# Seven half-token products for eight in the last gate and the output projection, with weights summed by accumulating DMAs

## The chip, the cores and the metric

The kernel runs on one core of a Trainium2 chip. The metric is device time in microseconds (us) of one execution, the median of several. TensorE (PE in the profile, its weight loads PEld), VectorE (DVE), ScalarE (ACT), GpSimd (POOL) and the DMA queues (issued by SP or by POOL) run side by side; each works through its own instructions in order.

## The reference

Two layers, 512 tokens, model width 1024. The part that the change touches is the gates, the merge and the output projection of each layer:

```python
h = _rmsnorm(x, g_mix[l])
proj = h @ w_in[l]                 # 4096 gate columns, then the inputs of the four branches
...                                # y_a conv module, y_b, y_c, y_d three attentions
ys = jnp.stack([y_a, y_b, y_c, y_d], axis=2)
branch = jnp.einsum('bsnc,ncd->bsnd', ys, w_branch[l])
gates = jax.nn.sigmoid(gate_pre.reshape(bsz, seq, N_BRANCH, D_MODEL) + gate_b[l])
mixed = jnp.sum(gates * branch, axis=2)
x = x + mixed @ w_out[l]
x = x + _conv_ffn(_rmsnorm(x, g_ffn[l]), w_up[l], ffn_conv_w[l], ffn_conv_b[l], w_down[l])
```

All of it is float32. The result has the shape of x.

## The kernel before

**Precision.** A float32 product is made of three: each operand is split into an upper part (hi, a rounded copy made by ScalarE) and a lower part (lo, the difference, made by VectorE), and TensorE adds hi x hi, hi x lo and lo x hi in PSUM (`prod`, L243 to L245). So every weight costs one ScalarE copy (L222) and one VectorE subtraction (L224), besides its DMA (L218).

**Weights.** They are packed on the host in units of 128 x 1024 floats (512 KB) in the order of use. `weights` (L197) loads a unit into one of two raw buffers, splits it into one of three hi and three lo buffers, and `unit` (L228) hands it out; the next unit is traced one ahead (`LOOK`), with a priority that lets it go before other work. A raw buffer is free again when the lower part has been made, a hi or lo buffer when TensorE has used it.

**Layout.** Activations lie transposed: channels on the partitions, the 512 tokens along the row. A block (`block`, L256) is one unit: 8 tiles of 128 input channels, three matmuls of 128 x 128 by 512 tokens each, 24 in all.

**The order in a layer.** Projections for the three attentions and the conv module come first, then four gates in the order 1, 2, 3, 0 (`ORDER`), then the output projection, the FFN's up-projection and its down-projection. Attention and the conv module run as generators in a side queue; `tick` (L844) takes one step of each of them, between blocks, so that their small matmuls stand among the large ones. In the third gate the queue still holds the end of attention and of the conv module; it is emptied after that gate.

**A gate** (`gates`, L797). For each of eight 128-channel tiles: a block, a multiplication by RB (the reciprocal norm of each token, L806), a tanh on ScalarE (L808). Two tiles later the branch product of 6 matmuls (`branch`, L818) and, on VectorE, (tanh + 1) times it (L835), which is added to the tile `mixed[d]` (L836), on POOL except for the last two tiles of the last gate. In the last gate `mixed[d]` is split at once into mh and ml (L840, L841), which are the moving operands of the output projection.

**The output projection** (`layer`, L1210). Eight blocks; the first two stop after six of eight input tiles and take the last two later, so that the last gate's tail is covered. Each result is added to the residual loaded from memory (`update`, L877: L882), stored as the new residual (L883), and turned into the FFN's input (`norm_tile`, L289: xh L300, xl L301, squares L309, their sum L310).

The down-projection already uses seven products for eight, with sums of weights that VectorE makes during the FFN and that go through memory (`weight_sums`, L973; L978 to L984). The gate and the output projection do not.

## Time and profile before

| | |
|---|---|
| median of 3 runs | 1558.79 us (1558.77 to 1559.04) |
| span of the profiled execution, first to last instruction | 1556.7 us |
| TensorE busy | 1550.7 us |
| weight loads busy | 1287.2 us |
| VectorE busy | 1235.9 us |
| ScalarE busy | 834.7 us |
| POOL busy | 174.8 us |
| DMA | 244.86 MB, 157 GB/s |

The page gives the span of the profiled execution and not its time outside the span; the median of the runs is 2.1 us above it. A matmul's duration in the profile includes its way through the array, and matmuls overlap, so a busy TensorE is not yet one at its peak: the distance from one start to the next is what counts. Weight loads run beside the matmuls. In a row on a group stand the line, engine, operation, what is written and read, shapes, count, then busy us and mean ns of one, then the idle time of that engine just ahead and what ended it. A row of the timeline begins with its start and its length in us.

### The profile page before, as it was taken

To read this page: it belongs to the slowest core of one execution; us is meant where nothing else is said; L and a number is where in the kernel's file an instruction comes from. 1 tells how busy PE (TensorE), PEld (TensorE's weight loads), DVE (VectorE), ACT (ScalarE), POOL (GpSimd) and SP (SyncE) were. 2 spreads that over 40 slices of the span, in tenths; PEclk is the share of its full clock that TensorE was granted. 3 is DMA by queue.
4 is the path that set the end of the run, shared out by engine and by line. 5 is a ranking of instruction groups with operands and counts; after the bars stand their busy time and mean duration, and the time that the engine had idled before them with its cause. 6 is when DMAs were issued, how large, how long until landed. Compare 5 with 4: busy or idle time off the path is not lost.

```text
span 1556.7 us, 20353 instructions
## 1 busy us (share of the span) xinstructions
PE 1550.7 (100%) x7122; PEld 1287.2 (83%) x7122; DVE 1235.9 (79%) x2102; ACT 834.7 (54%) x1420; POOL 174.8 (11%) x304
## 2 busy tenths in 40 slices
PE   9999999999999999999999999999999999999999
PEld 8888888888888888888888888888888888888887
DVE  6689988765689997796676899887656899977964
ACT  6778767333445443364457787672434444443643
POOL 0102002122001111100001020022120111111000
PEclk9999999999999999999999999999999999999999
DMA  7632222222645555576555422223226667655674
GB/s 236 192 93 87 83 81 82 95 98 93 215 162 203 192 187 187 202 238 211 188 181 184 117 72 87 74 76 108 95 95 211 194 221 238 202 203 191 219 231 165
DMA packets 103382, 244.86 MB, mean 157 GB/s; under 512 B 27504, under 2 KB 29424, under 8 KB 103280
## 3 DMA queue, kind: packets, MB, share of 16 engines
q1 hardware_dynamic: 89392, 196.37, 39.6%
q0 software_dynamic: 13600, 46.67, 8.5%
q8 instruction: 56, 0.92, 0.2%
q10 hardware_dynamic: 288, 0.52, 0.1%
q14 instruction: 46, 0.38, 0.1%
HBM read 202.63 MB, written 35.66 MB: 153 GB/s over the span
## 4 chain that ended last, share of the span: by engine, by line
PE 94%; DVE 3%; ACT 3%; issue 0%; ACTq 0%; DVEq 0%
PE mm L243 22%; PE mm L244 22%; PE mm L245 22%; PE aux L1048 3%; PE aux L1047 3%; PE aux L1046 3%; PE mm L467 2%; PE mm L469 2%; PE mm L468 2%; PE mm L1047 2%; PE mm L1048 2%; PE mm L1046 2%; PE aux L760 2%; PE aux L737 2%; PE aux L467 1%; PE aux L469 1%
## 5 line engine op out<-in xcount | busy, mean ns | idle before, releaser
L222 ACT ACTIVATE w_hi<-w_raw 128x1024 fp32r<-128x1024 f32 (+1 forms) x305 | 318.6, 1045 | 382.6 <-PE mm L244 218.9
L243 PE MATMUL mm<-xh,w_hi 128*128 128x512 f32 x1280 | 499.5, 390 | 0.0
L244 PE MATMUL mm<-xl,w_hi 128*128 128x512 f32 x1280 | 498.6, 390 | 0.0
L245 PE MATMUL mm<-xh,w_lo 128*128 128x512 f32 x1280 | 498.6, 390 | 0.0
L224 DVE TENSOR_TENSOR w_lo<-w_raw,w_hi 128x1024 fp32r<-128x1024 f32 (+1 forms) x305 | 368.7, 1210 | 83.4 <-ACT w_hi L222 81.3
L245 PEld LDWEIGHTS mm<-xh,w_lo 128*128 128x128 f32 x1280 | 240.3, 188 | 50.7
L243 PEld LDWEIGHTS mm<-xh,w_hi 128*128 128x128 f32 x1280 | 240.3, 188 | 49.1
L244 PEld LDWEIGHTS mm<-xl,w_hi 128*128 128x128 f32 x1280 | 240.3, 188 | 48.7
L836 POOL TENSOR_TENSOR mx<-mx,t 128x512 f32<-128x512 f32 x44 | 66.9, 1530 | 428.0 <-DVE t L835 327.1
L405 DVE SCALAR_TENSOR_TENSOR cv<-cv,prm 128x512 f32<-128x512 f32 x120 | 93.8, 781 | 0.7
L915 DVE TENSOR_TENSOR U<-mm,RB 128x512 f32<-128x512 f32 x88 | 60.0, 686 | 34.9 <-PE mm L245 34.8
L918 ACT ACTIVATE cy<-U,prm 128x512 f32<-128x512 f32 x88 | 70.7, 807 | 30.1 <-DVE U L915 29.9
L806 DVE TENSOR_TENSOR t<-mm,RB 128x512 f32<-128x512 f32 x64 | 43.9, 686 | 47.0 <-PE mm L245 46.8
L467 PE MATMUL mm<-w_hi,xh 128*128 128x512 f32 x192 | 76.4, 398 | 0.4 <-DVE V L595 0.4
L468 PE MATMUL mm<-w_lo,xh 128*128 128x512 f32 x192 | 75.0, 390 | 0.0
L469 PE MATMUL mm<-w_hi,xl 128*128 128x512 f32 x192 | 74.8, 390 | 0.0
L724 ACT ACTIVATE e<-e,rl 128x256 f32<-128x256 f32 (+2 forms) x96 | 57.3, 597 | 21.8 <-DVE rl L723 21.5
L920 DVE SCALAR_TENSOR_TENSOR cy<-U,prm,cy 128x512 f32<-128x512 f32 x88 | 65.5, 746 | 1.3
L919 DVE SCALAR_TENSOR_TENSOR cy<-U,prm,cy 128x512 f32<-128x512 f32 x88 | 65.3, 744 | 0.6 <-ACT cy L918 0.6
L924 ACT ACTIVATE fth<-cy 128x512 f32<-128x512 f32 x44 | 27.8, 632 | 64.1 <-DVE cy L920 64.0
L984 POOL DMA_DIRECT2D sums<-t x44 | 23.9, 544 | 339.4 <-DVE t L978 311.3
L717 ACT ACTIVATE e<-e,nm 128x256 f32<-128x256 f32 (+2 forms) x96 | 57.6, 600 | 2.7
(300 smaller groups left out, 2605.2 us busy)
## 6 DMA issues: line engine op xcount, KB each, us to landing
w_raw<-W SPq DMA_DIRECT2D x223, 512.0 KB, 3.5
quad<-W POOLq DMA_DIRECT2D x44, 512.0 KB, 5.3
w_raw<-W SPq DMA_DIRECT2D x66, 256.0 KB, 3.6
sums<-t POOLq DMA_DIRECT2D x44, 256.0 KB, 3.2
sums<-quad POOLq DMA_DIRECT2D x44, 256.0 KB, 3.8
w_raw<-sums SPq DMA_DIRECT2D x44, 256.0 KB, 3.8
w_raw<-sums SPq DMA_DIRECT2D x22, 512.0 KB, 4.4
res<-xn SPq DMA_DIRECT2D x24, 256.0 KB, 2.0
```

Of the source, the lines that this page charges most:

```text
L222: w = nc.scalar.activation(hi[:, s], raw[:, s], AF.Copy)
L224: nc.vector.tensor_tensor(lo[:, s], raw[:, s], hi[:, s].bitcast(F32), ALU.subtract)
L243: mm(ps, lhsT=wh, rhs=xh, start=start, stop=False)
L244: mm(ps, lhsT=wh, rhs=xl, start=False, stop=False)
L245: self.last_mm = mm(ps, lhsT=wl, rhs=xh, start=False, stop=stop)
L405: self.after_mm(v.scalar_tensor_tensor(acc, u[:, t:t + S], w(t), acc, ALU.mult, ALU.add))
L467: mm(pss[b], lhsT=self.Xh[k][:, t], rhs=hi[:, s], start=k == 0, stop=False)
L468: mm(pss[b], lhsT=self.Xh[k][:, t], rhs=lo[:, s], start=False, stop=False)
L469: self.last_mm = mm(pss[b], lhsT=self.Xl[k][:, t], rhs=hi[:, s], start=False, stop=k == KT - 1)
L1046: mm(ps, lhsT=x[0], rhs=w[0][:, cols], start=start, stop=False, skip_group_check=again)
L1047: mm(ps, lhsT=x[0], rhs=w[1][:, cols], start=False, stop=False, skip_group_check=again)
L1048: self.last_mm = mm(ps, lhsT=x[1], rhs=w[0][:, cols], start=False, stop=stop, skip_group_check=again)
```

## The change

The matrix product of the last gate (weights of gate 0, named `0`) and that of the output projection (`o`) are each cut in two halves of output channels, `a` and `b`, which gives four groups: `0a`, `0b`, `oa`, `ob`. In a group the weights are a 2 x 2 block matrix (output half by input parity) and the input is one too (input parity by token half). Seven products of sums of such blocks (S1 to S4, A11, A12, A22) replace the eight plain block products. Each product is one 512 KB unit of weights and 24 matmuls over 256 tokens.

- The sums of weights are made by DMA: a chain tile is loaded with one block and three others are added to it one after the other by accumulating DMAs from POOL (`grow`), and the splits for S3, S2 and S4 are taken between; A22's raw tile grows into that for S1. The two chain tiles (a, b) belong to the new pool `outp`.
- The sums of inputs are made by VectorE: `input_forms` reads the residual again, applies the gain and makes four forms from each of four pairs of tiles, beside the third gate; `mixed_forms` does it for each pair of tiles of `mixed`.
- The results are recombined by ScalarE copies and VectorE adds (`seven_copy`, `seven_sum`), then `last_gate` applies RB and tanh, `last_out` adds the residual and goes on to `norm_tile`.
- `LAST` is the order of all products and the two branch units. The first three of the output projection do half of their input tiles, then the other half.
- The pool of attention closes after the third tile of the third gate instead of after that gate, and `outp` opens there. `th` has four buffers instead of three. The adds of `mixed` in the last gate go to VectorE from tile 4 on.
- The whole residual (two tiles to a buffer, shared with the sums) is loaded after the last branch products.

```diff
+LAST = [('0a', n) for n in ('S3', 'A11', 'A22', 'S2', 'A12', 'S1')] + [
+    ('0b', 'S3'), ('0a', 'S4'), ('0b', 'A11'), ('branch', 0), ('0b', 'A22'), ('0b', 'S2'), ('0b', 'A12'), ('0b', 'S1'),
+    ('branch', 1), ('0b', 'S4'),
+    ('oa', 'S3'), ('oa', 'A11'), ('oa', 'A12'), ('oa', 'A22'), ('oa', 'S2'), ('ob', 'S3'), ('oa', 'S1'), ('ob', 'A11'),
+    ('oa', 'S4'), ('ob', 'A22'), ('ob', 'S2'), ('ob', 'A12'), ('ob', 'S1'), ('ob', 'S4')]
+CHAINS = {'0a': ('0b', 'S3', 'A22'), '0b': ('oa', 'A11', 'S2'), 'oa': ('ob', 'S3', 'A12'), 'ob': (None, '', '')}
...
+    def grow(self, raw, src):
+        self.nc.gpsimd.dma_start(raw, src, accum_op=ALU.add)
+    def chain_start(self, l, key):
+        raw = self.op.tile([P, 1024], F32, name="chain", tag=f"chain{key[1]}", bufs=1)
+        self.nc.sync.dma_start(raw, self.quarters[l][key, 1, 0])
+        self.chains[key] = raw
+    def seven_unit(self, l, key, n):
...
+        if n[0] == 'S':
+            raw = self.chains[key] if n != 'S1' else self.others[key]
+        else:
+            raw = self.wpool.tile([P, 1024], F32, name="w_raw", tag="w_raw", bufs=2)
+            nc.sync.dma_start(raw, q[key, int(n[1]) - 1, int(n[2]) - 1])
...
+        nc.scalar.activation(hi, raw, AF.Copy)
+        nc.vector.tensor_tensor(lo, raw, hi.bitcast(F32), ALU.subtract)
+        add = {'S3': (1, 1), 'A22': (1, 0), 'S2': (0, 1)}.get(n)
+        if add:
+            self.after.append(lambda: self.grow(raw, q[(key,) + add]))
+        if n == 'A22':
+            self.others[key] = raw
+        key2, at, then = CHAINS[key]
+        if n == at:
+            self.chain_start(l, key2)
+        if n == then:
+            self.after.append(lambda: self.grow(self.chains[key2], q[key2, 0, 0]))
+        return hi, lo
...
-        (v if n == ORDER[3] and d >= 6 else nc.gpsimd).tensor_tensor(m, m, t, ALU.add)
-        if n == ORDER[3]:
-            mh = self.op.tile([P, S], F32R, name=f"mh{d}", tag=f"mh{d}", bufs=1)
-            ml = self.op.tile([P, S], F32R, name=f"ml{d}", tag=f"ml{d}", bufs=1)
-            nc.scalar.activation(mh, m, AF.Copy, scale=0.5)
-            v.scalar_tensor_tensor(ml, m, 0.5, mh.bitcast(F32), ALU.mult, ALU.subtract)
-            self.MH.append((mh, ml))
+        (v if n == ORDER[3] and d >= 4 else nc.gpsimd).tensor_tensor(m, m, t, ALU.add)
+        if n == ORDER[3] and d % 2 == 1:
+            self.mixed_forms(d // 2)
...
+    def form_sums(self, t, b11, b12, b21, b22):
+        t1, t2, t3, t4 = (t[:, n * 256:(n + 1) * 256] for n in range(4))
+        p = self.nc.vector.tensor_tensor
+        p(t3, b12, b22, ALU.subtract)
+        p(t1, b11, b12, ALU.subtract)
+        p(t2, t3, b11, ALU.subtract)
+        p(t4, b21, t2, ALU.add)
...
+    def mixed_forms(self, j):
...
+        for h, l, s in ((th, tl, t), (bh[:, :256], bl[:, :256], x[:, :256]), (bh[:, 256:], bl[:, 256:], y)):
+            nc.scalar.activation(h, s, AF.Copy, scale=0.5)
+            v.scalar_tensor_tensor(l, s, 0.5, h.bitcast(F32), ALU.mult, ALU.subtract)
...
+    def seven_part(self, key, n, w, js, e):
+        ps = self.seven_bank(key, n)
+        o = ps[:, e * 256:(e + 1) * 256]
+        for j in js:
+            s = slice((2 * j + e) * P, (2 * j + e + 1) * P)
+            xh, xl = self.seven_x(key, n, j)
+            for i, (a, x) in enumerate(((w[0], xh), (w[0], xl), (w[1], xh))):
...
+                self.last_mm = self.nc.tensor.matmul(o, lhsT=a[:, s], rhs=x, start=start, stop=j == 3 and i == 2,
+                                                     skip_group_check=True)
...
+    def seven(self, key, n, done):
+        w = self.unit()
+        for e in range(2):
+            self.seven_part(key, n, w, range(4), e)
...
+        if n in ('S3', 'A11'):
+            self.seven_copy(key, n)
+            return
+        if not (key == 'ob' and n == 'S1'):
+            self.seven_sum(key, n)
+        done(key, n)
...
+    def last_gate_and_out(self):
...
+        for key, n in steps[:at]:
+            if key == 'branch':
+                bu = self.unit()
+                for d in range(4 * n, 4 * n + (4, 2)[n]):
+                    self.branch(ORDER[3], d, bu, self.ths[d])
+                    self.tick()
+                continue
+            self.seven(key, n, self.last_gate)
+        for d in (6, 7):
+            self.branch(ORDER[3], d, bu, self.ths[d])
+        for q in range(4):
+            self.load_residual(q)
...
+        for key, n in steps[at:at + 3]:
+            ws.append(self.unit())
+            for e in range(2):
+                self.seven_part(key, n, ws[-1], (0, 1), e)
+        for (key, n), w in zip(steps[at:at + 3], ws):
+            for e in range(2):
+                self.seven_part(key, n, w, (2, 3), e)
...
+        for key, n in steps[at + 3:]:
+            self.seven(key, n, self.last_out)
...
-                for n in ORDER[:3]:
-                    self.gates(n)
+                for n in ORDER[:2]:
+                    for _ in self.gates(n):
+                        pass
+                third = self.gates(ORDER[2])
+                next(third)
+                while any(g is not conv for g in self.side):
+                    self.tick()
+            with tc.tile_pool(name="outp", bufs=1, reuse_waits="tile") as self.op:
+                self.chains, self.others = {}, {}
+                self.input_forms()
+                self.chain_start(l, '0a')
+                self.after.append(lambda: self.grow(self.chains['0a'], self.quarters[l]['0a', 0, 0]))
+                for _ in third:
+                    pass
                 while self.side:
                     self.tick()
-            with tc.tile_pool(name="outp", bufs=1, reuse_waits="tile") as self.op:
-                self.gates(ORDER[3])
...
+                self.last_gate_and_out()
                 self.broadcast_norm()
```

More of the change, by code (lines that the diff above doesn't have):

```diff
@@ L88, in weight_units @@
                 units.append(('branch', (n, d // 4), 1024))
-    for d in range(8):
-        units.append(('out', d, 1024))
+    units.extend(('quarter', (key, r, c), 1024) for key in ('0a', '0b', 'oa', 'ob') for r in range(2) for c in range(2))
+    units.extend(('branch', (ORDER[3], h), 1024) for h in range(2))
     for i in range(NF):
@@ L201, in weights @@
             n, pieces = self.w_list[self.w_emitted]
+            after, self.after = self.after, []
+            with self.tc.high_priority(offset=ahead):
+                for f in after:
+                    f()
+            if n == 'seven':
+                with self.tc.high_priority(offset=ahead):
+                    self.w_ready.append(self.seven_unit(*pieces))
+                self.w_emitted += 1
+                continue
             with self.tc.high_priority(offset=ahead):
@@ new lines, in seven_x @@
+    def seven_x(self, key, n, j):
+        form = {'S1': 0, 'S2': 1, 'S3': 2, 'A22': 3}.get(n)
+        if form is not None:
+            return [t[:, form * 256:(form + 1) * 256] for t in (self.forms[j] if key[0] == '0' else self.mforms[j][0])]
+        if key[0] == 'o':
+            c = ('A11', 'A12', 'S4').index(n)
+            return [t[:, c * 256:(c + 1) * 256] for t in self.mforms[j][1]]
+        k, h = {'A11': (0, 0), 'A12': (1, 0), 'S4': (1, 1)}[n]
+        return [t[2 * j + k][:, h * 256:(h + 1) * 256] for t in (self.Xh, self.Xl)]
@@ L1157, in run @@
                         quads.append(src)
-                    else:
-                        self.w_list.append((n, lambda src=src: [src]))
+                    elif kind == 'quarter':
+                        quarters[a] = src
+                    elif kind == 'branch' and a[0] == ORDER[3]:
+                        branches.append(src)
+                    else:
+                        (held if kind == 'up' else self.w_list).append((n, lambda src=src: [src]))
+                for key, n in LAST:
+                    if key == 'branch':
+                        self.w_list.append((1024, lambda src=branches[n]: [src]))
+                    else:
+                        self.w_list.append(('seven', (l, key, n)))
+                self.w_list.extend(held)
+                self.quarters.append(quarters)
                 self.quads.append(quads)
```

167 lines of the change are left out of this document (141 added, 26 removed).

## The prediction, made before the result was known

> **What bounds the kernel now.** I read the page first (busy time, chain), then busy time by stretch, then matmul starts, then the groups of instructions of the two stretches that the change rewrites, then the DMA.
>
> ```profile
> span 1556.7 us, 20353 instructions
> PE 1550.7 (100%) x7122; PEld 1287.2 (83%) x7122; DVE 1235.9 (79%) x2102; ACT 834.7 (54%) x1420; POOL 174.8 (11%) x304
> PE 94%; DVE 3%; ACT 3%; issue 0%; ACTq 0%; DVEq 0%
> ```
>
> TensorE is never idle and carries 94% of the chain that ended last. Time can go only where TensorE has less to stream, and only as long as no other engine becomes late. The profile's span is 1556.7 us; the median of the runs is 1558.79, so 2.1 us lie around the span. I work out differences and put them on 1558.8.
>
> ```profile
> core 0: us, PE busy (x) PEld busy (x) DVE busy (x) ACT busy (x) POOL busy (x), PEclk, DMA share, GB/s
> 276.00:342.00 66.00, 66.00 (x303) 54.69 (x303) 48.88 (x77) 24.28 (x32) 16.37 (x11) 1.00 0.30 102
> 342.00:390.00 48.00, 48.00 (x214) 39.74 (x213) 23.99 (x29) 16.29 (x21) 8.59 (x6) 1.00 0.30 95
> 390.00:434.00 44.00, 44.00 (x196) 36.44 (x195) 27.03 (x35) 18.95 (x26) 1.47 (x10) 1.00 0.61 202
> 434.00:460.00 26.00, 26.00 (x117) 21.52 (x116) 23.95 (x37) 10.40 (x13) 3.26 (x6) 1.00 0.52 182
> ```
>
> These are, in layer 0, the third gate, the last gate, the output projection and the start of the FFN; layer 1 has the same stages. VectorE (DVE) is half idle in the last gate, 61% busy in the output projection and 92% busy in the FFN, where TensorE still does not wait. The granted clock is 1.00 throughout.
>
> **The products: what TensorE saves.** Before, the last gate and the output projection are 8 blocks each of 24 matmuls over 512 tokens: 384 in a layer. After, four groups of seven products, each 24 matmuls over 256 tokens: 672 in a layer. Half as wide is not half as long by itself, because each matmul brings its own 128x128 weight load. The attention's value products are the nearest case that the trace has: 256 wide, each with its own load, several in a row.
>
> ```profile
> 82.89 0.39 PE L243 MATMUL mm<-xh,w_hi 128*128 128x512 f32 x1
> 83.12 0.39 PE L244 MATMUL mm<-xl,w_hi 128*128 128x512 f32 x1
> 83.35 0.39 PE L245 MATMUL mm<-xh,w_lo 128*128 128x512 f32 x1
> 83.57 0.63 PE L760 MATMUL aux<-pt,V 128*128 128x256 f32 x4
> 84.05 0.27 PE L737 MATMUL aux<-cst,e 128*128 128x128 f32 x1
> ...
> 83.12 0.19 PEld L245 LDWEIGHTS mm<-xh,w_lo 128*128 128x128 f32 x1
> 83.35 0.65 PEld L760 LDWEIGHTS aux<-pt,V 128*128 128x128 f32 x4
> ```
>
> The duration (0.39) is a latency; what counts is the distance of starts. From 82.89 to 83.57 are three 512-wide starts, 0.227 us each. From 83.57 to 84.05 are four 256-wide ones, 0.120 each. So 384 x 0.227 = 87.2 us become 672 x 0.120 = 80.6: 6.6 us less in a layer, 13.2 in both. The ends: at exactly half of 0.227 the products take 76.3 and save 10.9 (21.8 in both). If all went as the widest gap that these rows allow (three distances inside the x4 row take 0.35, so the fourth takes 0.13), they take 87.4 and save nothing. I take 0.120, the mean of a run of four; weight loads start 0.11 to 0.12 apart there, so the load is what paces them.
>
> In a sentence apart: the Trainium skill, TensorE: Matmul & The Clock Gate, Back-to-back issue gap, gives N/2.4 + 2.5 ns at full clock, that is an estimated 216 ns for 512 and 109 ns for 256, and by it the layer would save 82.9 - 73.4 = 9.5 us; the rows above show 227 and 120, 11 ns more at either width, and the measurement decides.
>
> **The VectorE sum.** Durations of its instructions and of the two it exchanges work with:
>
> ```profile
> L224 DVE TENSOR_TENSOR w_lo<-w_raw,w_hi 128x1024 fp32r<-128x1024 f32 x9 | 11.0, 1224 | 1.6 <-ACT w_hi L222 1.5
> L806 DVE TENSOR_TENSOR t<-mm,RB 128x512 f32<-128x512 f32 x7 | 4.8, 692 | 12.1 <-PE mm L245 12.1
> L835 DVE SCALAR_TENSOR_TENSOR t<-th,mm 128x512 f32<-128x512 f32 x7 | 4.8, 682 | 0.0
> L841 DVE SCALAR_TENSOR_TENSOR ml<-mx,mh 128x512 fp32r<-128x512 f32 x5 | 3.5, 693 | 10.4 <-ACT mh L840 10.4
> ...
> L301 DVE SCALAR_TENSOR_TENSOR xl<-xn,prm,xh 128x512 fp32r<-128x512 f32 x7 | 5.2, 747 | 0.8 <-ACT xh L300 0.8
> ...
> L222 ACT ACTIVATE w_hi<-w_raw 128x1024 fp32r<-128x1024 f32 x8 | 8.5, 1060 | 15.6 <-PE mm L244 15.6
> L808 ACT ACTIVATE th<-t,gbh 128x512 f32<-128x512 f32 x8 | 5.7, 712 | 0.0
> ...
> 285.77 0.43 DVE L745 TENSOR_TENSOR pt<-aux,pt 128x256 fp32r<-128x256 f32 x1
> 319.12 2.35 DVE L224 TENSOR_TENSOR w_lo<-w_raw,w_hi 128x1024 fp32r<-128x1024 f32 x2
> 388.68 1.30 POOL L836 TENSOR_TENSOR mx<-mx,t 128x512 f32<-128x512 f32 x1 [5.52 <-DVE t L835]
> 389.31 1.22 DVE L836 TENSOR_TENSOR mx<-mx,t 128x512 f32<-128x512 f32 x1
> 389.67 0.39 PE L243 MATMUL mm<-mh,w_hi 128*128 128x512 f32 x1
> 393.62 0.68 DVE L836 TENSOR_TENSOR mx<-mx,t 128x512 f32<-128x512 f32 x1
> 395.01 0.69 DVE L841 SCALAR_TENSOR_TENSOR ml<-mx,mh 128x512 fp32r<-128x512 f32 x1 [0.70 <-ACT mh L840]
> ```
>
> Two w_lo back to back take 2.35, so instructions follow each other some 0.09 closer than their durations: 1.14 us at 1024 wide, 0.60 at 512, 0.34 at 256. What is added in a layer: 12 more weight splits (28 products and 2 branch units for 18 units), 16 small subtractions for the forms of the gate's input and 16 for those of the mixed sum, the recombination (three 512-wide instructions in each of four groups), four adds that leave POOL; the eight mh/ml splits become wider ones. By the rates above: 13.7 + 10.9 + 4.6 (lower parts of the input forms) + 7.2 + 2.4 + 3.6, some 42 us of VectorE in a layer. Stage by stage:
>
> Input forms (third gate): 4 x (4 x 0.34 + 1.14) = 10.0 us on VectorE, 8 x 0.71 + 4 x 1.06 = 9.9 on ScalarE. The stretch 276 to 342 leaves 17 and 42 us free: nothing on the path; without that cover the 10 us would fall on the next stage. The 2.1 MB that it loads once more meet a DMA share of 0.30.
>
> Attention's pool closing in the third gate:
>
> ```profile
> 293.14 0.69 DVE L780 TENSOR_TENSOR yl<-yf,yh 128x512 fp32r<-128x512 f32 x1
> ...
> 295.48 0.69 DVE L806 TENSOR_TENSOR t<-mm,RB 128x512 f32<-128x512 f32 x1 [0.99 <-PE mm L245]
> ```
>
> The last result of attention stands at 293.8, before the third block of this gate is read at 295.48. That gate's first branch needs it anyway, so emptying the side queue there drains nothing: 0.
>
> The last gate's second half is where the sum does not close. Between the first branch product and the second half of the output's first product (which needs the forms of the last mixed pair), TensorE has seven further branch products (7 x 6 x 0.227 = 9.5), five products of 24 x 0.120 = 2.9 (14.4), the first halves of three (36 x 0.120 = 4.3) and three matmuls (0.4): 28.6 us. In that time VectorE must do eight gate multiplies of L835's kind (8 x 0.60 = 4.8), four adds (2.4), the 16 subtractions (5.4), four 1024-wide lower parts (4.6), three pairs of 256 and 512 wide (2.8), seven weight splits (8.0; the ring of three lets none be made sooner), three recombinations (1.8) and four RB multiplies (2.4): 32.2. So 3.6 us are missing in each layer even if VectorE never idles: 7.2 in both. Before, the same hand-over had room: the last ml ends at 395.7, while 36 matmuls from 389.7 last to 397.9. Ends for this term: 0, if TensorE's own slower pitch absorbs it; 7.7 a layer by rival two.
>
> In the output projection VectorE has, for a group, 7 x 1.14 + 3 x 0.60 + 4 x 0.60 (residual) + 4 x 0.66 (xl) + 4 x 0.60 (sqacc) = 17.2 us in 7 x 2.88 = 20.2: 85%, below the 92% at which the FFN runs without a wait. ScalarE: 7 x 1.06 for splits, three copies and eight xh and sq at 0.71 at most: 15.2. I cost both at 0. Without cover each late split costs at most its 1.14. After the last product two half-width adds replace one add; the FFN's first block reads that tile in its last quarter: 0.
>
> The waits that are added, and the queues: each accumulating DMA waits on POOL for both halves of the split that reads its tile. Behind it on POOL stand the gate's adds for tiles 0 to 3, used two products later, and the next accumulation. On SP, the residual loads into XR2 and XR3 wait until the last forms are read (they share those tiles); a weight load or a store that stands behind them waits too, at most the 3.6 us above again. The buffers of raw weights: of two, one is held from A22 to S1, three products; loads, splits and that hold fill about 28 of 40 buffer-us in a group: 0.
>
> ```profile
> DMA packets 3384, 8.90 MB, mean 202 GB/s; under 512 B 384, under 2 KB 384, under 8 KB 3381
> w_raw<-W SPq DMA_DIRECT2D x8, 512.0 KB, 4.2
> ...
> quad<-W POOLq DMA_DIRECT2D x44, 512.0 KB, 5.3
> ```
>
> The first two rows are of 390 to 434. The trace has no accumulating DMA. Nearest is POOL's plain 512 KB load, 5.3 us to landing. From the split of S3 to that of S2 three products pass, 8.6 us, less 2.3 for the split itself: 6.3, so 5.3 fits; twice that (10.6) fits only with the two products of lead that the ring allows (5.8). Between 0 and 4.3 us each, seen three times in a group; I take 0, the row it is nearest to, and leave the rest to rival three.
>
> Sum: 1558.8 - 13.2 + 7.2 = 1552.8 us.
>
> **Rivals.**
> One, the narrow matmuls go at half of 0.227. Then 21.8 is saved, the stretch above is shorter on TensorE by 159 x 0.0065 = 1.0, so 4.6 a layer comes back: 1558.8 - 21.8 + 9.2 = 1546.2. Against it: the run of four.
>
> Two, no measurable change: VectorE's backlog is larger. The rows at 388.68 and 389.31 show an add, which takes 0.68 at 393.62, take 1.22 on VectorE while POOL runs its own; four such meetings in the stretch are 2.2 us. At its end come two hops over ScalarE (two half-wide tanh, by L808's 0.71 an estimated 0.4 each, then the upper part of the last form, 1.06) with little left for VectorE to do: 1.9. 3.6 + 2.2 + 1.9 = 7.7 a layer: 1558.8 - 13.2 + 15.4 = 1561.0. For it: every term has a row. Against it: the hops can be filled with weight splits.
>
> Three, slower: the DMA becomes the bound of the output projection. In 40.3 us it must move some 15 weight transfers (7.9 MB), residual loads and stores (4.2) and the FFN's first quads (1.0): 13.1 MB, 325 GB/s. The stretch before moved 8.90 MB at a share of 0.61 in 44 us, 331 GB/s if full. If the seven accumulations in it (3.7 MB) cost double because the destination is read as well, 16.8 MB need 50.7 us, 10.4 more a layer: 1552.8 + 20.8 = 1573.6. It decides from about 1.3 times the price of a plain load, where the stage grows by 3 us and the gain is gone. Against it: a part is prefetched in the last gate, where the share was 0.30, and stores can trail into the FFN, so half the price (1563) is as likely as all of it.
> The Trainium skill, Collectives: The Full Stack, The bandwidth ceiling, says that an adding transfer is slow for its two source reads, not for the add, and so runs at about half the rate of a copy; no run here shows it yet, and by that rule this rival's time is the one above.
>
> Four, the change does not do what it says: loads of 0.19 us stay in front of each narrow matmul, 672 x 0.19 = 128 us, 1640. The four starts in 0.48 us speak against it.
>
> **How the numbers follow.** Forecast 0.39, rival one 0.11, two 0.21, three 0.26, four 0.01; 0.02 for anything else. A measurement of this kernel tells 0.2%, 3.1 us, from no change, so faster is below 1555.7 and slower above 1561.9. The forecast and rival one are faster; some of the forecast's spread (a backlog of 5 a layer) lies within: faster 0.46, same 0.21, slower 0.33. The range goes from rival one to rival three, 1546 to 1573; the forecast's own is 1549 to 1557.
>
> **What would show it.** Starts of the 256-wide products 0.120 apart (0.113: rival one). VectorE over 95% busy from the first branch of the last gate on, and TensorE waiting for the forms of the last mixed pair, some 3.6 us. No wait of ScalarE's w_hi for a DMA, accumulations landing within about 6 us; w_hi waiting for the chain tile and DMA slices at 9 in the output projection would be rival three. I am wrong if VectorE's order differs from need so that splits come ahead of forms, or if the accumulation is much dearer than a load.

## The result, and the profile after

The changed kernel takes 1608.61 us (median of 4 runs, 1607.47 to 1609.09) against 1558.91 beside it: ratio 1.0317, 95% interval 1.0303 to 1.0332. The forecast was 1552.8, its range ended at 1573, so it was wrong in sign and by 56 us. First the page after: span, busy times, shares of the chain that ended last.

```profile
span 1607.0 us, 21849 instructions
PE 1564.0 (97%) x7698; PEld 1319.2 (82%) x7698; DVE 1322.6 (82%) x2236; ACT 898.4 (56%) x1516; POOL 199.5 (12%) x332
PE 80%; DVE 11%; ACT 4%; DMA 2%; issue 2%; POOL 0%; SPq 0%; ACTq 0%; DVEq 0%
```

TensorE falls from 94 to 80% of the chain, VectorE rises from 3 to 11 and DMA appears. Busy time by stretch in layer 0 (third gate, last gate, output projection, start of the FFN):

```profile
core 0: us, PE busy (x) PEld busy (x) DVE busy (x) ACT busy (x) POOL busy (x), PEclk, DMA share, GB/s
276.00:342.00 66.00, 62.06 (x283) 51.19 (x282) 56.38 (x95) 31.61 (x42) 17.57 (x13) 0.97 0.55 165
342.00:396.00 54.00, 52.24 (x388) 49.38 (x387) 42.15 (x52) 29.72 (x44) 15.13 (x14) 1.00 0.69 161
396.00:442.00 46.00, 41.09 (x294) 38.89 (x293) 34.88 (x49) 23.74 (x33) 5.65 (x15) 0.89 0.72 184
442.00:484.00 42.00, 33.63 (x156) 27.28 (x156) 32.44 (x49) 16.85 (x21) 3.27 (x6) 0.96 0.56 185
```

TensorE was busy in every microsecond of these stretches before; now 3.9, 1.8, 4.9 and 8.4 us are missing, and the granted clock is below 1.00 in three of them. Two accounts of the 50.3 us between the spans (1607.0 - 1556.7) close, the second to some 2 us:

| place, by the starts of matmuls | before | after | us |
|---|---|---|---|
| start to the first product of the mixed sum, layer 0 | 389.7 | 395.1 | +5.4 |
| from there to the down-projection, layer 0 | 283.3 | 301.9 | +18.6 |
| down-projection of layer 0 to the first product of the mixed sum, layer 1 | 491.7 | 496.7 | +5.0 |
| from there to the down-projection, layer 1 | 283.3 | 304.5 | +21.2 |

By kind, over all pairs of successive matmuls: a distance within 12 ns of the even pitch (0.227 us at 512 wide, 0.120 at 256) counts as work, one within 12 ns of the pitch at half clock (0.427 at 512 wide, as the rows of the last section show it, 0.213 at 256) as halved clock, and what goes beyond the even pitch otherwise as waiting. Waiting grew by some 49 us, halved clock by some 12; less the 13.2 saved that is some 48. A distance can be near 0.427 or 0.213 by chance, so the rule is sure only where the granted clock is below 1.00; that is 0.986 on the mean here and 0.999 before. The waits stand in the third gate (4.1 us at 323.9, 3.7 in layer 1), between 375 and 413 (some 10 in each layer), at 441.8 (5.3; 3.3) and at 475.8 (3.3; 4.2).

**Third gate.** TensorE stood before the convolution's second transposes (instructions of VectorE and TensorE; the two rows above the line of dots are of the kernel before, the rest of the one after):

```profile
313.23 1.27 DVE L425 TENSOR_SCALAR ms<-mv 128x4 f32<-128x4 f32 x1
316.51 0.16 DVE L277 SCALAR_TENSOR_TENSOR rln<-rs_q,rln 128x4 f32<-128x4 f32 x1
...
318.03 1.26 DVE L482 TENSOR_SCALAR ms<-mv 128x4 f32<-128x4 f32 x1
319.20 0.41 DVE L903 TENSOR_TENSOR sums<-xf 128x256 f32<-128x256 f32 x1
325.53 1.21 DVE L929 TENSOR_TENSOR form<-sums,form 128x1024 fp32r<-128x1024 f32 x1
327.44 0.16 DVE L334 SCALAR_TENSOR_TENSOR rln<-rs_q,rln 128x4 f32<-128x4 f32 x1
328.23 0.69 PE L500 MATMUL aux<-cst,cv 128*128 128x128 f32 x2 [3.94 <-DVE cv L491]
```

The serial chain for a reciprocal root on 128x4 elements took 3.4 us before (313.23 to 316.67) and takes 9.6 now (318.03 to 327.60): input sums, lower parts and weight splits stand between its links.

**Mixed hand-over.** Busy time in stretches of the kernel after (columns as above; the first reaches from the end of the first branch product to the first matmul that needs the lower part of the last form), then two instructions of VectorE:

```profile
368.55:410.49 41.94, 36.30 (x227) 32.02 (x225) 38.81 (x57) 21.31 (x31) 8.72 (x8) 0.92 0.58 141
372.20:405.00 32.80, 28.25 (x194) 25.23 (x192) 32.80 (x49) 17.99 (x27) 5.59 (x5) 0.97 0.63 161
400.00:405.00 5.00, 2.48 (x11) 1.76 (x11) 5.00 (x10) 2.28 (x5) 0.00 (x0) 0.79 0.54 193
405.00:410.00 5.00, 4.40 (x18) 3.78 (x17) 3.18 (x5) 2.95 (x3) 0.40 (x1) 0.53 0.00 0
...
408.07 1.23 DVE L272 TENSOR_TENSOR w_lo<-w_raw,w_hi 128x1024 fp32r<-128x1024 f32 x1 [1.82 <-ACT w_hi L271]
409.22 1.22 DVE L949 SCALAR_TENSOR_TENSOR mform<-sums,mform 128x1024 fp32r<-128x1024 f32 x1
```

VectorE has no idle time from 372.2 to 405, while TensorE waits for it (28.25 of 32.80 us busy). At the end the order works against it too: the lower part of the last form (409.22) stands behind a weight split that waits 1.82 us for ScalarE, which waits for a buffer that TensorE holds. From 405 to 410 the clock is 0.53.

**Hand-over to the FFN.** Two waits of 440 to 480 after, the end of the norm's chain before (450.68) and after (476.70), and TensorE's wait for a bank of PSUM:

```profile
PE mm L300 <- ACT w_hi L245: 5.1, 1, 5.1
ACT w_hi L245 <- DMA w_raw<-W: 6.1, 1, 6.1
...
450.68 0.68 DVE L277 SCALAR_TENSOR_TENSOR RB<-rs_q,RB 128x512 f32<-128x512 f32 x1
476.70 0.69 DVE L334 SCALAR_TENSOR_TENSOR RB<-rs_q,RB 128x512 f32<-128x512 f32 x1
479.28 0.47 PE L300 MATMUL mm<-xh,w_hi 128*128 128x512 f32 x1 [3.14 <-DVE U L1181]
```

The FFN's first product stands ahead of the last two output products on TensorE, and its weight is late. It is late because of what is loaded beside it. The stretch from 432 to 444 and the load of this weight, in the kernel after and below the dots in e11, which has no accumulating loads:

```profile
432.00:444.00 12.00, 10.05 (x84) 9.85 (x83) 9.37 (x13) 5.87 (x8) 2.19 (x11) 1.00 0.96 284
w_raw<-W SPq DMA_DIRECT2D x1, 512.0 KB, 11.3
...
432.00:444.00 12.00, 11.44 (x92) 10.91 (x91) 11.46 (x16) 7.00 (x9) 0.00 (x0) 1.00 0.40 133
w_raw<-W SPq DMA_DIRECT2D x1, 512.0 KB, 3.5
```

The weight is issued at 434.6 and lands 11.3 us later; in e11 it is issued at 435.0 and lands in 3.5. In the kernel after, the two loads of the FFN's quads (512 KB each, the weights whose sums the down-projection needs) stand behind the accumulating loads on POOL's queue and start at 433.6 and 434.1, beside the last accumulation and the stores; in e11 they start at 406.3 and 406.9. So the DMA share is 0.96 there, against 0.38 in the same stretch of the kernel before.

The norm's chain ends 22.4 us after the last output product (454.95), before 18.4 (432.97), and the FFN's fifth product waits for it.

### The profile page after: what moved, and what is told of

The parts are those of the page before. It is cut to its first block, busy times and chain, and to the rows that moved or that the text cites. A ratio compares the mean times of both kernels' runs of the same rounds, so it can differ in the third digit from the quotient of the medians.

```text
span 1607.0 us, 21849 instructions
## 1 busy us (share of the span) xinstructions
PE 1564.0 (97%) x7698; PEld 1319.2 (82%) x7698; DVE 1322.6 (82%) x2236; ACT 898.4 (56%) x1516; POOL 199.5 (12%) x332
## 3 DMA queue, kind: packets, MB, share of 16 engines
q1 hardware_dynamic: 91696, 200.57, 39.4%
## 4 chain that ended last, share of the span: by engine, by line
PE 80%; DVE 11%; ACT 4%; DMA 2%; issue 2%; POOL 0%; SPq 0%; ACTq 0%; DVEq 0%
PE mm L302 15%; PE mm L300 15%; PE mm L301 15%; PE aux L972 6%; PE aux L1312 2%; PE aux L1313 2%; PE aux L1314 2%; PE mm L524 2%; PE mm L526 2%; PE mm L525 2%; DVE w_lo L247 2%; PE mm L1313 2%; PE mm L1312 2%; PE mm L1314 2%; PE aux L817 2%
## 5 line engine op out<-in xcount | busy, mean ns | idle before, releaser
L300 PE MATMUL mm<-xh,w_hi 128*128 128x512 f32 x1152 | 451.3, 392 | 15.4 <-ACT w_hi L245 8.2
L302 PE MATMUL mm<-xh,w_lo 128*128 128x512 f32 x1152 | 450.8, 391 | 0.6 <-DVE w_lo L247 0.5
L301 PE MATMUL mm<-xl,w_hi 128*128 128x512 f32 x1152 | 450.5, 391 | 0.0
L245 ACT ACTIVATE w_hi<-w_raw 128x1024 fp32r<-128x1024 f32 (+1 forms) x273 | 284.9, 1044 | 288.5 <-PE mm L301 104.4
L247 DVE TENSOR_TENSOR w_lo<-w_raw,w_hi 128x1024 fp32r<-128x1024 f32 (+1 forms) x273 | 329.7, 1209 | 88.1 <-ACT w_hi L245 84.9
L300 PEld LDWEIGHTS mm<-xh,w_hi 128*128 128x128 f32 x1152 | 217.4, 189 | 61.0 <-ACT w_hi L245 8.6
L302 PEld LDWEIGHTS mm<-xh,w_lo 128*128 128x128 f32 x1152 | 217.2, 189 | 47.3 <-DVE w_lo L247 1.8
L301 PEld LDWEIGHTS mm<-xl,w_hi 128*128 128x128 f32 x1152 | 217.4, 189 | 43.7 <-DVE xl L358 0.2
L272 DVE TENSOR_TENSOR w_lo<-w_raw,w_hi 128x1024 fp32r<-128x1024 f32 x32 | 41.8, 1306 | 23.9 <-ACT w_hi L271 23.7
L972 PE MATMUL aux<-mform,w_hi 128*128 128x256 f32 x256 | 53.9, 309 | 5.8 <-DVE mform L949 2.1
```

The costliest lines, as they stand in the source:

```text
L245: w = nc.scalar.activation(hi[:, s], raw[:, s], AF.Copy)
L247: nc.vector.tensor_tensor(lo[:, s], raw[:, s], hi[:, s].bitcast(F32), ALU.subtract)
L300: mm(ps, lhsT=wh, rhs=xh, start=start, stop=False)
L301: mm(ps, lhsT=wh, rhs=xl, start=False, stop=False)
L302: self.last_mm = mm(ps, lhsT=wl, rhs=xh, start=False, stop=stop)
L972: self.last_mm = self.nc.tensor.matmul(o, lhsT=a[:, s], rhs=x, start=start, stop=j == 3 and i == 2, skip_group_check=True)
```

## Experiments

All are edits of the changed kernel; the ratio is to the kernel before, run beside it. e8, e10, e11 and e17 leave out work that the result needs: they measure what it costs and are no candidates.

| run | edit | us | ratio (95%) |
|---|---|---|---|
| e1_gate7 | the gate alone in seven | 1566.25 | 1.0038 (1.0025 to 1.0051) |
| e2_out7 | the output alone in seven | 1591.86 | 1.0207 (1.0191 to 1.0222) |
| e3_order | FFN behind the last product | 1608.16 | 1.0306 (1.0289 to 1.0323) |
| e4_conv | convolution's chain first | 1609.28 | 1.0320 (1.0305 to 1.0336) |
| e5_own | own tile for A22 | 1609.17 | 1.0324 (1.0309 to 1.0340) |
| e6_own_order | e3 and e5 | 1603.75 | 1.0291 (1.0276 to 1.0306) |
| e7_forms_mid | forms written later | 1606.21 | 1.0302 (1.0284 to 1.0319) |
| e8_nosums | mixed forms without their sums | 1588.04 | 1.0185 (1.0170 to 1.0200) |
| e9_behind | forms behind the convolution | 1623.17 | 1.0411 (1.0395 to 1.0426) |
| e10_plain_load | plain loads, nothing is added | 1602.57 | 1.0278 (1.0262 to 1.0293) |
| e11_no_load | no accumulating loads | 1593.44 | 1.0225 (1.0208 to 1.0242) |
| e12_gate7_behind | e1 and e9 | 1581.42 | 1.0141 (1.0125 to 1.0156) |
| e13_gate7_split | e1, forms split 2 and 2 | 1558.18 | 0.9995 (0.9985 to 1.0004) |
| e14_gate7_split_a11 | e13, A11 first | 1568.23 | 1.0051 (1.0033 to 1.0069) |
| e15_half_norm | e6, norm by half tiles | 1601.41 | 1.0281 (1.0261 to 1.0301) |
| e16_all | all orders and tiles together | 1611.01 | 1.0332 (1.0316 to 1.0347) |
| e17_account | e13's split, e8 and e11 | 1567.33 | 1.0051 (1.0034 to 1.0067) |
| e18_pool_sums | half of the mixed sums on POOL | 1614.28 | 1.0351 (1.0335 to 1.0367) |

**The two halves of the change.** e1 ends the list of products before the output and puts the old output back; e2 the reverse.

```diff
-                for key, n in LAST:
+                for key, n in LAST[:-14]:     # e1; e2: LAST[-14:]
```

> Only the last gate is taken in seven products (with the input's forms in the third gate, and attention's pool closing there); the output projection is in eight again, with plain loads. Theory A, VectorE's work is put where it delays others at three places (the third gate's convolution, the hand-over of the mixed sum, the hand-over to the FFN): this kernel keeps the first place alone. Of the changed kernel's stretches the third gate was 5.5 us a layer longer and the last gate 0.55 shorter, so some 5.0 a layer: 1558.9 + 10 = 1569, between 1564 and 1574. Theory B, the loss hangs on the seven output products and their accumulating loads alone, and the gate's part is sound: 6.6 us less than before (two gates of 3.3 us), 1552.

> Only the output projection is taken in seven products; the last gate is in eight again, nothing is formed of the input, and attention's pool closes where it did. Theory A: the two later places stay, 18.5 and 21.2 us of the changed kernel's loss by stretches, less what the half-token gate took of the hand-over: 1558.9 + 35 to 40 = 1594 to 1599, and with the gate-only kernel the two parts add up to the changed kernel within some 4 us. Theory B': the two parts hurt only together (VectorE is full when both are there): each of them alone is below 1565.

The gate costs 6.9 us, the output 32.5, together 39.4 of 49.7. Theory A has e1 in its range; e2 ends 2 us below it, and since 10 us arise only when both halves are there, "within some 4 us" missed. At least half of these 10 stand at the mixed hand-over: from 375 to 425, in layer 0, TensorE waits 5.3 us in e2, 10.3 in the changed kernel.

**The hand-over to the FFN, by order and buffer.**

```diff
+            self.behind = end if i < 2 else None      # e3: an order without a wait, for every matmul of these blocks
-            raw = self.wpool.tile([P, 1024], F32, name="w_raw", tag="w_raw", bufs=2)
+            pool, tag, bufs = (self.op, "chaina", 1) if (key, n) == ('ob', 'A22') else (self.wpool, "w_raw", 2)   # e5
+            raw = pool.tile([P, 1024], F32, name="w_raw", tag=tag, bufs=bufs)
```

> On TensorE's queue the first four products of the FFN are held behind the last product of the output projection; in the changed kernel the FFN's first product stands ahead of the last two there. Theory A1, the order is the cause at the third place: the waits at 441.8 (5.3 us; 3.3 in layer 1) and 475.8 (3.3; 4.2) go with their cold clock, 16 to 20 us: 1589 to 1593. Theory A2, the first weight of the FFN comes late whatever the order, since its raw buffer is held by the grown A22: the wait moves behind the last product and stays; only the later wait for a bank becomes shorter: 1600 to 1605. Theory C, the bank wait is set by VectorE's load alone: 1605 to 1609.

> The grown A22 of the last group gets a tile of its own, so that no buffer of the ring of raw weights is held for three products and the FFN's first weight is loaded some 8 us sooner. Theory A2 (the order of TensorE is harmless; VectorE, which works in order, stands behind the split of the FFN's first weight, and that weight's load starts when A22's buffer comes free and lands 9 us later): the wait at 441.8 (5.3 us; 3.3 in layer 1) goes, with it the cold clock behind it and a part of the later bank wait: 10 to 18 us, 1591 to 1599. Theory E, the load is late because the DMA queues are full there, whenever it is issued: 1605 to 1609.

> The tile of its own for A22 and the FFN's first four products behind the last output product, both. Theory A2: the order adds nothing to the own tile for the first wait; the bank wait (3.3 and 4.2 us) goes only if the norm's chain starts sooner, which the order brings, so 1586 to 1594, 3 to 6 below the own tile alone. Theory A2', the norm's chain is stretched on VectorE by weight splits put between its links, whatever is ahead: equal to the own tile alone within 2 us.

Neither alone moves the time, both together 4.9 us: A1 fell, and A2 as well. In e3 the wait only moved in among the last output products (6.1 us at 442); its time lies in theory C's range, but the order did shorten the bank wait (to 1.1 and 3.1 us), which C excludes. Theory E has the full DMA right (0.96 above) and "whenever it is issued" wrong: in e5 the FFN's first weight is issued at 425.0 and lands in 4.2 us. Waits of e6 from 425 to 455:

```profile
ACT w_hi L273 <- DMA w_raw<-W: 4.9, 1, 4.9
PE aux L981 <- DVE sv L1030: 4.8, 2, 4.2
```

With both edits the FFN's weight no longer counts. Now the split for S1 waits for the accumulation on A22 (issued at 433.2, landed at 439.0), and TensorE for a small sum (sv) that stands behind two weight splits on VectorE.

**The accumulating loads.**

```diff
-        self.nc.gpsimd.dma_start(raw, src, accum_op=ALU.add)
+        self.nc.gpsimd.dma_start(raw, src)      # e10; e11: nothing
```

> The accumulating DMAs are plain loads of the same bytes into the same tiles on the same queue: nothing is added, so the chained weights hold the last quarter loaded instead of a sum. Theory H (what an accumulation costs is its price over a plain load, 6.4 against 5.2 us): 5 to 10 us less, 1599 to 1603. Theory I (the price does not matter; what matters is that a load starts only after the split that reads the tile, and the next split waits for it): within 3 us of the changed kernel, 1606 to 1611.

> The accumulating DMAs are left out altogether, so the chained weights are never summed and all four products of a chain use the quarter loaded first. Theory I: with no load between two splits of a tile, the wait at the hand-over to the FFN (5.3 and 3.3 us, then 3.3 and 4.2 for a bank) shrinks, and the late splits of the whole output projection too: 10 to 20 us less, 1589 to 1599. Theory J (VectorE's order and load alone make those waits): within 4 us of the changed kernel, 1605 to 1611.

The price over a plain load is 6.0 us of the time (H), and the load itself, added or not, 9.1 more: 15.2 in all (in I's range). Issue groups of the kernel after and of e10 for the 24 loads into chain tiles, median us to landing last (the 8 into A22's tiles take 5.7 and 3.8):

```profile
chain<-W POOLq DMA_DIRECT2D x24, 512.0 KB, 6.4
...
chain<-W POOLq DMA_DIRECT2D x24, 512.0 KB, 4.5
```

In e11 the wait at 441.8 is gone (0.7 stays); the bank wait (3.3 and 4.2) is not. In e10, with plain loads on the same queue, the FFN's quads start at 432.5 and 3.3 us of that wait stay (2.4 in layer 1). So some 4 of the 9.1 us hang on what POOL's queue holds back, rather than on the way from split to split that theory I names. This is read from the rows; a run that starts the quads sooner and keeps the accumulations was not made.

**VectorE at the mixed hand-over.**

```diff
-        self.form_sums(t, x[:, :256], x[:, 256:], y[:, :256], y[:, 256:])      # e8: x and y are split in place of t
+        self.form_sums(t, x[:, :256], x[:, 256:], y[:, :256], y[:, 256:], nc.gpsimd if j < 2 else None)      # e18
```

> The mixed sum's forms leave out their 16 subtractions and adds: two of the halves are split in place of the four sums (5.4 us of VectorE less in a layer, all else as it was). Theory A (VectorE's backlog makes the waits at 399 to 413, 7.0 us and 2.8 of cold clock in layer 0, 6.9 and 3.1 in layer 1): 5.4 us a layer and most of the cold clock go, 12 to 16 us: 1593 to 1597. Theory G (the hops over ScalarE or the order of the splits make them, not the amount): below 5 us, 1603 to 1609.

> Of the mixed forms' 16 subtractions and adds, the eight of the first two pairs go to POOL, all else as in the changed kernel. Theory M (POOL relieves VectorE: 2.7 us less in a layer, half of what the run without the sums saved): 1597 to 1601. Theory N (an instruction on POOL stretches those on VectorE beside it, as the row of the add that took 1.22 in place of 0.68 had it, so the relief is paid back; and the sums come later): 1606 to 1613.

10.8 us less of VectorE (32 instructions by 0.34) give 20.6 us (A, more than expected): from 400 to 425 waiting falls from 7.0 to 1.1 us, and the granted clock of this stretch is 1.00, where 2.8 us of halved clock were. The edit does two things more: the sums are also gone from the path between a mixed tile and its split, and the tiles are free that the residual loads wait for (they start at 311.8 to 322.0 in place of 401.6 to 410.8). No run separates the three. POOL is no way out: the time rises by 5.7 us, N's direction, 1.3 beyond its range. Two instructions of e18, on VectorE and on POOL:

```profile
370.47 5.62 DVE L949 SCALAR_TENSOR_TENSOR mpart<-mx,mpart 128x256 fp32r<-128x256 f32 x1
374.77 1.04 POOL L906 TENSOR_TENSOR sums<-mx,sums 128x256 f32<-128x256 f32 x1
```

One lower part, which takes 0.41 alone, lasts 5.62 us, as long as POOL's string of instructions runs beside it: six of them without a gap, the last of which ends at 375.8.

**The third gate.** e4 gives the convolution's chain a priority, e7 writes the forms after it in the program; e9 and e12 put the forms' subtractions behind it on VectorE's queue (an order, no wait); e13 does that for the last two pairs of forms only.

```diff
+            while j == 2 and self.un is None:      # e13: two pairs free, two behind; e9, e12: all behind
+                yield
+            if self.un is not None and len(self.forms) >= 2:
+                self.tc.add_manual_dep(r.ins, self.un.ins.name, info, reason="pace")
```

> The convolution's short chain on VectorE (statistics, reciprocal root, normalising) goes ahead of the input's forms, by priority. Theory A: the wait of TensorE for it in the third gate (4.1 us at 323.9, 3.7 in layer 1) goes with its cold clock: 1608.6 - 8 to 12 = 1597 to 1601. Theory D: VectorE has no room at all in this stretch, and the forms come late for the last gate in its place: 1606 to 1610.

> The input's forms are made only after the convolution's normalising, 10 us of VectorE later in the third gate. Theory F (the scheduler fills each gap of the convolution's serial chain with a long instruction as long as one is ready; priority alone could not help): with nothing ready the chain is short again, the wait at 323.9 (4.1; 3.7 in layer 1) goes with its follow-ups, 8 to 12 us: 1597 to 1601. Theory D (VectorE is full to the end of the third gate): the forms are late for the last gate's first product by as much, 1606 to 1611.

> The earlier run with the forms after the convolution changed only the order in which the program was written; VectorE's queue still had them among the convolution's chain. Here an order without a wait puts the input's subtractions and adds behind the normalising on VectorE's queue. Theory F (long instructions filled into the gaps of a serial chain stretch it from 3.5 to 9 us): the chain is short again, the wait in the third gate (4.1 and 3.7 us, with 1 to 2 us of small ones and cold clock behind each) goes: 8 to 13 us, 1596 to 1601. Theory D (VectorE has no room before the last gate): the forms become late there instead, 1606 to 1611.

> The last gate alone in seven products (1566.25 us in the first set), with the input's forms behind the convolution's normalising on VectorE's queue. Theory F: its two waits for the convolution (3.9 and 4.6 us, with 1.6 to 2 of small ones and 1.3 cold behind each) go, 12 to 14 us, and what is left is the saving of its products: 1559 - 6.6 = 1552 to 1555, faster than the kernel before. Theory D: 1563 to 1568.

> The last gate alone in seven products; of the input's four pairs of forms the first two are made where VectorE was idle (300 to 310) and the last two behind the convolution's normalising. Theory F2 (both earlier placements were wrong by where they put the work: all four ahead of the convolution delay its chain by 9 us, all four behind it are 10 us late for the gate): 5 us fit on each side, the waits of both kinds shrink to 0 to 2 us a layer, 1553 to 1558. Theory D2 (the stretch from 310 to 350 has not enough idle time on VectorE for any placement): between 1562 and 1575, one of the two waits remains.

e4 and e7 left the forms inside the chain on VectorE and say little (1609.3 and 1606.2). e9 and e12 made the chain short, and the time 15 us longer, so theory F as first put fell: the forms were now late for the gate. That is D's direction, 12 and 13 us beyond its ranges. Stretches of e12, and below the dots two of the kernel before (columns as above):

```profile
300.00:310.00 10.00, 10.00 (x51) 8.35 (x49) 4.04 (x5) 2.92 (x5) 2.20 (x2) 1.00 0.95 294
330.00:340.00 10.00, 6.80 (x32) 5.41 (x30) 10.00 (x15) 5.30 (x7) 4.13 (x4) 1.00 0.36 57
...
300.00:310.00 10.00, 10.00 (x50) 8.35 (x50) 4.56 (x6) 2.80 (x4) 1.94 (x2) 1.00 0.20 64
310.00:320.00 10.00, 10.00 (x45) 8.25 (x44) 9.55 (x28) 3.46 (x4) 1.29 (x1) 1.00 0.15 52
```

In e12 VectorE idles 6 us from 300 to 310 and is full from 320 to 340, where TensorE begins to wait (6.80 of 10 us busy). Two pairs of forms fit ahead of the chain and two behind. With that (e13) the chain is whole, 3.5 us:

```profile
316.78 1.28 DVE L484 TENSOR_SCALAR ms<-mv 128x4 f32<-128x4 f32 x1
320.07 0.16 DVE L336 SCALAR_TENSOR_TENSOR rln<-rs_q,rln 128x4 f32<-128x4 f32 x1
```

The gate in seven is then level with the kernel before: 8.1 us less than e1, by the place of 10 us a layer of VectorE alone. It is not faster (expected 1553 to 1558): distances of matmuls beyond the even pitch still add up to 6 to 7 us more than in the kernel before, about the 6.6 saved. None of it is clock, which is 1.00 throughout.

**More of the same kind.** e14 changes the order of products, e15 makes the norm's parts per half tile, e16 joins these with e3 and e5, takes the output's first three products in three parts and puts the last pair's forms first.

```diff
-LAST = [('0a', n) for n in ('S3', 'A11', 'A22', 'S2', 'A12', 'S1')] + [
+LAST = [('0a', n) for n in ('A11', 'S3', 'A12', 'A22', 'S2')] + [      # e14, e16
-            self.norm_tile(d, xn, self.op)
+            self.norm_half(d, xn, h)                                        # e15, e16: 256 columns, at every product
```

> The same, and the gate's first product is A11, which takes the input itself, so the forms are wanted 2.9 us later; S1 and S4 of the first group move behind a product of the second. Theory F2: no worse than the run beside it by more than 1 us, and up to 4 us a layer better where the forms were still late: 1551 to 1556. Theory D2: 1558 to 1570.

> The changed kernel with the own tile for A22 and the FFN behind the last product (1603.75 us together), and with the norm's input parts and squares made for half tiles, as each product gives them, instead of for four whole tiles after the last two products. Theory K (the wait for a bank comes from the norm's chain, which ended 22.4 us after the last product against 18.3 before, since four tiles' parts and squares, some 5 us of VectorE, fall behind the last products): that wait (1.1 and 1.6 us in that kernel, 3.3 and 4.2 in the changed one) goes, 1596 to 1601. Theory L (twice as many half-wide instructions with their fixed parts fill VectorE in the output's last group, and splits come later still): 1603 to 1610.

> All together on the changed kernel: forms split around the convolution, A11 first, the half norm, the FFN behind the last product, the own tile for A22, the output's first three products in three parts instead of two (the last mixed pair is wanted 2.2 us later), and that pair's forms first on VectorE. By theory A (each place has its own wait, and each edit takes its own): third gate 10 less, mixed hand-over 5 to 10 less, FFN hand-over 8 to 12 less: 1576 to 1586. If VectorE's amount alone counts, waits move and the gain is below 10: 1598 to 1608.

e14 is 10 us worse than e13, in D2's range and outside F2's; new waits are of 2.9 us at 341.8 and 3.1 at 380.3. In e15 the bank wait went from e6's 1.1 and 1.6 us to 0.2 and 1.1, but the median fell by 2.3 us only, to 0.4 above K's range, and the runs of the two overlap (1601.1 to 1608.0, 1602.6 to 1607.7): 2.7 and 2.6 us of waiting stand at 441.6 and 445.8, among the last output products, in the run profiled, the slowest of its four (1607.95). e16 gains nothing and lies above both ranges: a wait of 6.0 us at 379.3 is new. Apart from e13, moving work about, with VectorE as full as it is, moved the waits.

**The account.**

```diff
+    # e17: the forms split as in e13, no sums in the mixed forms as in e8, no accumulating loads as in e11
```

> The changed kernel with the input's forms split around the convolution, without the sums of the mixed forms (halves split in their place) and without the accumulating loads (the chained weights are never summed). If the three causes are separate, the gains add: 1608.6 - 8 - 20.6 - 15.2 = 1565, between 1560 and 1570. If they share waits (one wait's end hides another), less than two thirds of that: above 1579. What stays then is the wait for a bank before the FFN's fifth product, 3.3 and 4.2 us, with its cold clock.

41.3 us less, where the three gains one by one make 43.9 (8.1, measured on e1, + 20.6 + 15.2): to within 3 us they add, as separate causes would. What stays, 7.9 us over the kernel before and with it the 13.2 saved, is for a little more than half the bank wait: 3.3 and 4.2 us, with 1.4 and 2.6 of halved clock. The rest is in small waits.

No version that does the whole work beats the kernel before by more than can be measured; e13 is level with it.

## Why the prediction was wrong, by its steps

**The products: right.** TensorE in the output projection after:

```profile
428.93 0.40 PE L972 MATMUL aux<-mpart,w_hi 128*128 128x256 f32 x2
429.17 0.28 PE L972 MATMUL aux<-mpart,w_lo 128*128 128x256 f32 x1
429.29 0.40 PE L972 MATMUL aux<-mpart,w_hi 128*128 128x256 f32 x2
```

Three distances from 428.93 to 429.29: 0.120 each, as taken, which makes 13.2 us saved by the sum. Rival one (half pitch) and four (loads in front) are out. That the weight load sets the pace, as the prediction says, is not shown: the 256 columns between the two widths take 0.107 us, so that 0.013 is left at either width, and an addition of this size to every matmul fits as well.

**Input forms, costed at 0: the step that failed first.** "The stretch 276 to 342 leaves 17 and 42 us free" is an average. The free time on VectorE lay at 300 to 310 and after 320; a part of the work fell between the links of a serial chain that TensorE waits for, where VectorE had been 96% busy (310 to 320). Its worth is 8.1 us by e1 and e13.

**Attention's pool closing earlier, 0:** nothing speaks against it (e13 has it and is level); by itself it was not tried.

**VectorE's backlog, 7.2 us: right in kind, too small.** The sum of 32.2 against 28.6 was the right one to make, but the stretch lasted 41.9 us in layer 0 (368.55 to 410.49 above), with VectorE busy for 38.8 of them. It did eight weight splits in it and the end of a ninth, not seven, one of them ahead of the last form (named as a way to be wrong); three instructions took 1.1 us more each beside an add of POOL (rival two: 1.50, 1.51 and 2.31 for 0.41, 0.41 and 1.21); and the clock halved. Taking away 10.8 us of VectorE, with what else e8 changes, gave back 20.6.

**Output projection and FFN start, 0: failed.** 85% was again an average. After the last two products come the parts and squares of four tiles, where before it was those of the last; the chain of the norm ended 4 us later, counted from the last output product, and the FFN waited 3.3 and 4.2 us. Most of this wait hangs on the order of the FFN's products (e6: 1.1 and 1.6); the half tiles of e15 take a part of what is left (0.2 and 1.1). What the two edits gain in time beyond the moved waits was not separated.

**Queues, 0 to 3.6: failed.** The prediction looked at what stands behind the accumulations on POOL's queue and left out the FFN's quads. They started 27 us later than without accumulations (e11) and filled the DMA just when the FFN's first weight was loaded: ScalarE waited 6.1 us for it, TensorE 5.3, and 3.3 in layer 1. The held raw buffer is not enough to explain it, since e11 holds it too and issues the weight at the same time; with a tile of its own for A22 the weight comes early, but another wait stood there (e5, 0; e6, 4.9).

**Accumulating DMAs, 0, between 0 and 4.3 each: the term was mis-sized.** The 32 of them (24 into chain tiles, 8 into A22's) cost 15.2 us (e11), 6.0 of it the add (e10); the late quads are a part of it. The slack of "8.6 less 2.3" supposed that a tile's split is made as soon as the ring allows; VectorE made it later: in e6 the lower part of the last A22 ended at 432.95, when its own product had begun (432.5). Rival three had the sign, and its mechanism at one place: the DMA share is 0.96 from 432 to 444, but 0.72 over the output projection, and plain loads bring 6.0 us, not 20.8. By the Trainium skill's rule on source reads (Collectives: The Full Stack, The bandwidth ceiling) an adding load would take twice a plain one, an estimated 9.0 us from e10's 4.5, if all of the time to landing were transfer; the trace has 6.4, and the measurement decides.

**The clock: not in the sum.** Some 12 us. A term for halved clock behind waits was missing altogether.

## What to carry to other kernels

A busy share over a long stretch does not cover added work: look for the place where it will stand, and for the serial chain or the in-order wait that it will stretch there; here the same 10 us a layer cost 8 us more in one place, and 23 more in another, than split over both (e1, e12, e13). When an engine without slack feeds TensorE, a microsecond added can cost more than itself, since the wait also costs clock (e8: 10.8 us of work and a shorter path to the split, 20.6 of time). If a weight is summed by a load, count the whole loop (split, issue, landing, next split), and what stands behind the load on its queue.

## What the hardware showed that was not expected

**The clock halves after waits.** TensorE in layer 1 of the kernel after, behind the bank wait:

```profile
1277.62 0.77 PE L300 MATMUL mm<-xh,w_hi 128*128 128x512 f32 x1 [4.06 <-DVE U L1181]
1278.18 0.63 PE L301 MATMUL mm<-xl,w_hi 128*128 128x512 f32 x1
1278.61 0.63 PE L302 MATMUL mm<-xh,w_lo 128*128 128x512 f32 x1
```

For 5 us starts are 0.43 apart in place of 0.227. The same behind a shorter wait, in e2 (a matmul, then the stretch behind the wait), and below the dots two stretches at the mixed hand-over of the kernel after:

```profile
469.35 0.77 PE L299 MATMUL mm<-xh,w_hi 128*128 128x512 f32 x1 [3.17 <-DVE U L1173]
468.50:475.30 6.80, 5.95 (x14) 4.73 (x15) 6.80 (x12) 4.96 (x6) 0.54 (x1) 0.50 0.53 161
...
399.50:402.90 3.40, 1.82 (x11) 1.21 (x10) 3.40 (x6) 1.73 (x3) 0.00 (x0) 1.00 0.59 171
402.90:409.70 6.80, 5.29 (x19) 4.35 (x19) 4.98 (x10) 3.76 (x5) 0.10 (x1) 0.50 0.20 70
```

The Trainium skill (TensorE: Matmul & The Clock Gate, What's actually happening) has half clock after an idle window of some 3.4 us that runs freely, not from the wait's start. The traces agree on the free run: 4.2 us halve it here, 3.3 at 475.8 (the row at 479.28 above; the granted clock is 1.00 from 472 to 485) do not, and 3.3 at 465.8 in e2 do. They do not show that TensorE must be idle for the whole window: from 398 to 416 there are twelve waits of at most 1.9 us, 8 us together, and some 30 matmuls at the half-clock pitch, and in the 3.4 us ahead of the first halving, 399.5 to 402.9, TensorE was busy for 1.82. How little work in a window halves the clock, no run here was made to find.

**POOL stops VectorE.** In the kernel after, one lower part of 128x256 meets POOL's add, the other does not:

```profile
374.50 1.51 DVE L949 SCALAR_TENSOR_TENSOR mpart<-mx,mpart 128x256 fp32r<-128x256 f32 x1
382.99 0.41 DVE L949 SCALAR_TENSOR_TENSOR mpart<-mx,mpart 128x256 fp32r<-128x256 f32 x1
```

The Trainium skill (SBUF — State Buffer, Who interferes with whom) calls the port pair that the two share an exclusive lock, and says that an instruction of VectorE with two inputs in SBUF contends with one of POOL that reads SBUF. The 1.51, and the 5.62 of e18, agree; in e18 VectorE did not come in between six instructions of POOL in a row.
